# First modulation by pairs of feature tiles, q from two token tiles, written engine orders up to the end of q

## The chip, the cores and the metric

The kernel runs on one core of a Trainium2 chip. Its engines are TensorE (PE in the profile, with PEld for the loads of its stationary operand), VectorE (DVE), ScalarE (ACT), GpSimd (POOL) and SyncE (SP), which here issues nearly all transfers. The metric is the time of one execution in microseconds (us); for a set of runs the median is given.

## The reference

One layer of a hybrid backbone is computed for 128 context tokens and 512 latent tokens, width 1024, all in float32. Cut to what matters here:

```
mod = silu(cond) @ w_ada + b_ada            # cond: c for latent, c_ctx for context tokens
sh1, sc1, g1, sh2, sc2, g2 = split(mod, 6)
h = rms(x, norm_mix) * (1 + sc1) + sh1
q, k, v, gb, gc, u = split(h @ w_in, ...)   # 512, 128, 128, 512, 512, 512 columns
attn = attention(rope(rms(q)), [ctx_k, rope(rms(k))], [ctx_v, v])
y_conv = gb * conv3(gc * u)
x = x + g1 * (concat(rms(attn), rms(y_conv)) @ w_out)
h2 = rms(x, norm_ffn) * (1 + sc2) + sh2
x = x + g2 * ((silu(gate) * up) @ w_down)   # gate, up = split(h2 @ w_gate_up)
```

The part that is changed runs from the first transfer to the last product of q: it needs `sh1` and `sc1`, `h`, and `h @ w_in` for the first 512 columns.

## The kernel before

The 640 tokens are five token tiles of 128: 0 to 3 are latent, 4 is the context. The 1024 features are eight feature tiles of 128, called k below. The products that carry precision are made of three: an operand is split into a high part of type fp32r and a low part that is the difference (`wh` and `wl` for weights, `hH` and `hL` for h), and `mm3` (lines 154 to 156) adds high × high, high × low and low × high. A *step* of q is one `mm3` of one feature tile and one token tile, 512 columns wide, into the token tile's own PSUM bank; there are 40.

Before q's first step, each x tile is loaded, squared and summed (`x_norm`: ScalarE), scaled by its inverse root (GpSimd's power, VectorE's multiply), transposed (`xT_do`: TensorE, eight times 128 by 128) and copied to `xT` by ScalarE and VectorE. The first modulation is computed for one feature tile at a time: `ada1_load` brings the 128 scale and 128 shift columns of `w_ada`, in two halves of four row blocks, into `af` tiles (four buffers); `ada1_mm` multiplies them with the conditioning vectors, four products side by side in strips of 32 columns (line 379), into 256 columns of PSUM, and copies the result to `res`; `ada1_mod` adds the strips with two small products against `sel` (line 428), and `mod_evict` makes the coefficients `modA` and `modB` on VectorE. `h_do` then computes `hF` from `xT` (ScalarE for the latent tokens, VectorE for the context) and splits it into `hH` (ScalarE) and `hL` (VectorE).

q's weights come as four loads of two feature tiles (`wf`, three buffers), split by ScalarE and VectorE into `wh` and `wl` (four buffers each, lines 150 and 151). k's and v's two loads and the conv's loads use the same rings.

The order of the work is set in several ways. TensorE's is the order in which the program is written, from the preparation on. On VectorE, ScalarE and GpSimd, a written order holds only for the string `P1PRE`; behind it, and on SP throughout, a scheduler places each instruction by priority (`early(...)` raises or lowers it). The letters of `P1PRE`: `rN` normalise x tile N, `xN` transpose it, `aN` the modulation's products for feature tile N, `mN` the small ones, `hNc` h for feature tile N, `qNt` a step, `w` a split of q's weights, `v`, `p`, `c` small constants. For feature tiles 1 to 7 the string `P1SEQ` says what stands in each round: the small products of the next feature tile, its h, the modulation's products of the one after, and the five steps.

After q, its five banks are copied to `of` (ScalarE four, VectorE one), and k, v, attention, conv, output projection and the feed-forward part follow.

Of the kernel before, what the change touches and what calls it, by code (L numbers as in the profile page):

```python
# [36 lines left out]
XTE = [0, 1, 0, 1, 1, 1, 0, 1, 1, 0]  # L37
# [39 lines left out]
AO = 6  # L77
# [9 lines left out]
LOADS = [0, 0, 0, 0, 2, 1, -1, 0, 3, 3, 2, 2]  # L87
# [3 lines left out]
def build(ctx, tc, x_prompt, x_sample, c, cache_k, cache_v, c_ctx, norm_mix, norm_ffn, w_ada, b_ada,  # L91
# [163 lines left out]
    def W(key):  # L255
        p = place[key]
        while not in_pre[0] and stream_at[0] < len(order):
            nxt = order[stream_at[0]][0][0]
            ahead = AO if nxt == "o" else AOP if nxt in ("g", "u", "op") else AHEAD
# [52 lines left out]

    crow = T("crow", (16, P))
# [3 lines left out]
    def ada1_load(k):  # L317

        out = []
        for h in range(2):  # L320
            wf = T("af", (P, 4, 2, P), F32, AFB)
            for i, col in enumerate((D + k * P, k * P)):
                sp.dma_start(wf[:, :, i], wa[:, 4 * h:4 * h + 4, col:col + P])
            out.append(wf)
            yield
        ada1[k] = out
        yield
# [13 lines left out]
    loads = itertools.chain(*(ada1_load(k) for k in range(KD)))  # L341
    ada1 = {}
# [70 lines left out]
    def ada1_mm(k):  # L413
        while k not in ada1:
            ada1_next(1)
        rp = PB((P, 256), tag="c")
        for h, wf in enumerate(ada1[k]):
            for i in range(4):
                cond_mm(rp, 4 * h + i, wf[:, i].rearrange("p a b -> p (a b)"))
        res = T("res", (P, 256), F32, 2)  # L420
        dve.tensor_copy(res, rp)
        ada1[k] = res

    def ada1_mod(k):
        res = ada1.pop(k)
        mp = PB((P, 2, 1, 2))
        for i in range(2):
            pe.matmul(mp[:, i, 0], res[:, i * P:(i + 1) * P], sel[:, 0:2], start=True, stop=True)
        mod_evict(0, k, 1, mp[:, 0], mp[:, 1])
# [3 lines left out]
    def xT_do(t):  # L433

        both = PS2() if t < XB else None
        tps = [both[:, i] if t < XB else PB() for i in range(2)]
# [4 lines left out]
        if t < XB:  # L441
            for k in range(KD):
                turn(k)
        for i, tp in enumerate(tps):
            if t >= XB:
                for k in range(4):
                    turn(4 * i + k)
# [8 lines left out]
    def h_do(k, cc):  # L456
        if k not in hF:
            hF[k] = T("hF", (P, TOK), F32, 2)
        s = (slice(0, 512), slice(512, TOK))[cc]
        a, b = modA[0][:, k, cc:cc + 1], modB[0][:, k, cc:cc + 1]  # L460
        if cc == 0:
            act.activation(hF[k][:, s], xT[:, k, s], AF.Identity, bias=b, scale=a)
        else:
            dve.tensor_scalar(hF[k][:, s], xT[:, k, s], a, b, ALU.mult, ALU.add)
        if k == 0:
            split(hH[k][:, s], hL[k][:, s], hF[k][:, s])
        elif cc == 1:
            split(hH[k], hL[k], hF[k])

    pe_order = tc.manual_schedule(engines={mybir.EngineType.PE})  # L470
    pe_order.__enter__()
# [16 lines left out]
    qacc = []  # L488

    def q_mm(k, t):  # L490
        if not qacc:
            qa, qb = PS2(), PS2()
            qacc.extend([qa[:, 0], qa[:, 1], qb[:, 0], qb[:, 1], PB(tag="c")])
# [18 lines left out]
    steps = {"r": x_norm, "c": late_consts, "w": lambda i: load_split(*deferred.pop(0)), "p": lambda i: rows2_load(), "x": xT_do, "v": lambda i: (vec_do, vec2_do)[i](), "m": ada1_mod, "a": ada1_mm}  # L512
    pre_order = tc.manual_schedule(engines={mybir.EngineType.DVE, mybir.EngineType.Activation, mybir.EngineType.Pool})
    pre_order.__enter__()
# [809 lines left out]
```

## Time and profile before

| | |
|---|---|
| median of three runs | 760.89 us (759.51 to 763.18) |
| the profiled execution | 762.66 us, of which the span from first to last instruction is 760.9 us |
| mean granted clock of TensorE | 0.993 of full speed |
| PE busy | 739.5 us, 97% of the span |
| DVE, ACT, POOL busy | 73%, 49%, 6% of the span |
| moved by DMA | 84.52 MB, 111 GB/s in the mean |

The page divides the span into 40 slices of 19 us; the changed part fills the first three and a little of the fourth. A row of a timeline gives the start, the duration, the engine, the line, what is written and read, and in brackets how long the engine was idle before and what ended that. Several alike are put together (x8).

### The profile page before, as it was taken

Reading aid. Unit: us, or ns where it says so; the run is one execution under the profiler, and the core shown is the slowest. Engines: PE = TensorE matmul, PEld = TensorE weight load, DVE = VectorE, ACT = ScalarE, POOL = GpSimd, SP = SyncE. Lnnn points to the kernel's source line nnn. Section 1 sums busy time; section 2 is a strip of 40 time slices with the busy share of each in tenths; the row PEclk is TensorE's granted clock in tenths of the full one; section 3 lists DMA queues with packets and bytes.
Section 4 is the critical chain, followed back from the end, with each engine's and each line's share of the span. In section 5 each row is a group of like instructions: output and inputs, shape, how many; then the busy total and the mean of one; then the engine's idle time right before and its main releaser. Section 6 shows DMA issues by size and latency. Waiting matters only on the chain.

```text
span 760.9 us, 11844 instructions
## 1 busy us (share of the span) xinstructions
PE 739.5 (97%) x4580; PEld 664.6 (87%) x4580; DVE 552.7 (73%) x1003; ACT 369.6 (49%) x715; POOL 43.1 (6%) x73
## 2 busy tenths in 40 slices
PE   4999999999999999999999999999999999999997
PEld 3768888989998887899898789998889998899986
DVE  5556987676666797779879678884578866788653
ACT  5345867666656444765552135553125541255410
POOL 3104301011010110100000000000000000000000
PEclk9899999999999999999999999999999999999999
DMA  9985132522433363031335223223113132222312
GB/s 289 293 233 158 38 118 91 173 91 91 160 104 93 130 249 111 1 112 56 86 111 179 83 62 103 79 89 113 53 56 110 58 112 67 73 86 82 111 56 84
DMA packets 102349, 84.52 MB, mean 111 GB/s; under 512 B 4526, under 2 KB 82674, under 8 KB 102292
## 3 DMA queue, kind: packets, MB, share of 16 engines
q1 hardware_dynamic: 100980, 83.39, 35.5%
q8 instruction: 36, 0.59, 0.3%
q10 hardware_dynamic: 1056, 0.26, 0.2%
q0 software_dynamic: 256, 0.11, 0.1%
q14 instruction: 21, 0.17, 0.1%
HBM read 79.68 MB, written 2.75 MB: 108 GB/s over the span
## 4 chain that ended last, share of the span: by engine, by line
PE 82%; DVE 8%; DMA 3%; ACT 2%; SPq 2%; issue 1%; POOL 1%; DVEq 0%; POOLq 0%
PE pf L154 17%; PE pf L156 16%; PE pf L155 16%; PE pc L677 3%; PE pc L678 3%; PE pc L679 3%; PE po L834 3%; PE ps L791 2%; PE ph L154 2%; PE pt L817 2%; PE ph L155 2%; PE ph L156 2%; PE pc L379 2%; DMA af<-in_w_ada_dram 2%; DMA wf<-in_w_gate_up_dram 1%
## 5 line engine op out<-in xcount | busy, mean ns | idle before, releaser
L150 ACT ACTIVATE wh<-wf 128x1024 fp32r<-128x1024 f32 (+1 forms) x76 | 64.1, 843 | 95.7 <-PE pf L156 61.8
L154 PE MATMUL pf<-wh,gT 128*128 128x512 f32 (+1 forms) x225 | 88.1, 392 | 0.0
L155 PE MATMUL pf<-wl,gT 128*128 128x512 f32 (+1 forms) x225 | 87.7, 390 | 0.0
L156 PE MATMUL pf<-wh,gT 128*128 128x512 f32 (+1 forms) x225 | 87.7, 390 | 0.0
L151 DVE TENSOR_TENSOR wl<-wf,wh 128x1024 fp32r<-128x1024 f32 (+1 forms) x42 | 49.4, 1175 | 29.1 <-ACT wh L150 26.3
L677 PE MATMUL pc<-hH,wh 128*128 128x320 f32 x192 | 61.1, 318 | 0.0
L678 PE MATMUL pc<-hL,wh 128*128 128x320 f32 x192 | 59.4, 310 | 0.0
L679 PE MATMUL pc<-hH,wl 128*128 128x320 f32 x192 | 59.4, 309 | 0.0
L155 PEld LDWEIGHTS pf<-wl,gT 128*128 128x128 f32 x225 | 42.2, 188 | 10.0 <-issue 0.2
L154 PEld LDWEIGHTS pf<-wh,gT 128*128 128x128 f32 x225 | 42.2, 188 | 9.9 <-ACT wh L150 0.2
L156 PEld LDWEIGHTS pf<-wh,gT 128*128 128x128 f32 x225 | 42.2, 188 | 9.8
L154 PE MATMUL pf<-T,wh 128*128 128x320 f32 x160 | 49.7, 311 | 0.5 <-ACT u L1154 0.5
L155 PE MATMUL pf<-T,wl 128*128 128x320 f32 x160 | 49.5, 309 | 0.0
L155 PE MATMUL pf<-T,wh 128*128 128x320 f32 x160 | 49.5, 309 | 0.0
L156 PE MATMUL pf<-T,wh 128*128 128x320 f32 x160 | 49.5, 309 | 0.0
L154 PE MATMUL pf<-T,wl 128*128 128x320 f32 x160 | 49.5, 309 | 0.0
L156 PE MATMUL pf<-T,wl 128*128 128x320 f32 x160 | 49.5, 309 | 0.0
L154 PE MATMUL pf<-B,wl 128*128 128x320 f32 x152 | 47.3, 311 | 0.1
L156 PE MATMUL pf<-B,wl 128*128 128x320 f32 x152 | 47.1, 310 | 0.0
L155 PE MATMUL pf<-B,wl 128*128 128x320 f32 x152 | 47.0, 309 | 0.0
L1233 DVE TENSOR_TENSOR dm<-pf,g 128x512 f32<-128x512 f32 (+1 forms) x41 | 27.7, 675 | 22.8 <-PE pf L156 22.6
L154 PE MATMUL pf<-B,wh 128*128 128x320 f32 x136 | 42.3, 311 | 1.5 <-DVE cu L1183 1.5
(293 smaller groups left out, 2023.9 us busy)
## 6 DMA issues: line engine op xcount, KB each, us to landing
wf<-in_w_gate_up_dram SPq DMA_DIRECT2D x44, 512.0 KB, 4.0
aw<-in_w_ada_dram SPq DMA_DIRECT2D x24, 512.0 KB, 4.7
wf<-in_w_down_dram SPq DMA_DIRECT2D x20, 512.0 KB, 3.4
wf<-in_w_in_dram SPq DMA_DIRECT2D x18, 512.0 KB, 6.1
af<-in_w_ada_dram SPq DMA_DIRECT2D x32, 256.0 KB, 6.0
x<-in_x_sample_dram SPq DMA_DIRECT2D x8, 512.0 KB, 4.8
wf<-in_w_out_dram SPq DMA_DIRECT2D x8, 512.0 KB, 3.9
wf<-in_w_ada_dram SPq DMA_DIRECT2D x8, 512.0 KB, 3.7
```

What stands on the lines that cost most here:

```text
L150: act.activation(hi, src, AF.Copy)
L151: dve.tensor_tensor(lo, src, f32(hi), ALU.subtract)
L154: pe.matmul(out, lh, rh, start=start, stop=False, skip_group_check=more)
L155: pe.matmul(out, lh, rl, start=False, stop=False, skip_group_check=more)
L156: pe.matmul(out, ll, rh, start=False, stop=stop, skip_group_check=more)
L379: pe.matmul(out[CG * g:CG * (g + 1)], cp[:, k], w, start=(k < 4), stop=(k >= KD - 4), skip_group_check=True)
L677: pe.matmul(acc, wh[:, k], hH[k][:, c0:c0 + n], start=(k == 0), stop=False)
L678: pe.matmul(acc, wh[:, k], hL[k][:, c0:c0 + n], start=False, stop=False)
L679: pe.matmul(acc, wl[:, k], hH[k][:, c0:c0 + n], start=False, stop=(k == KD - 1))
L791: pe.matmul(s2[:, g, :320], q, kk[:, v, P + g * 320:P + (g + 1) * 320], start=(i == 0), stop=(i == 1))
L834: pe.matmul(ov, w, x[:, i].rearrange("p a q -> p (a q)"), start=(g == 0 and i == 0 and n == 0), stop=(last and i == len(kts) - 1 and n == 1))
L1233: dve.tensor_tensor(dm, ps[:, :n], g2[cc][:, oc], ALU.mult)
```

## The change

- **Modulation by pairs.** `ada1_load` brings the columns of two feature tiles at once (256 columns each of scale and shift), in halves of 1 MB; `ada1_mm` is written half by half and fills 512 columns of PSUM; `ada1_mod` makes the coefficients of both tiles with four small products. There are four pairs; the `af` ring still has four buffers, each twice as large.
- **h.** ScalarE writes `hH` directly from `xT`, and VectorE computes `hF` for all tokens and then `hL`. For feature tiles 0 and 1 this is done in parts: tokens 0 and 1 together (`a`), token tiles 2 (`b`), 3 (`c`) and 4.
- **Order of loads and steps.** Two x tiles come first, then the first pair's weights, q's first weights, and the other three x tiles. q begins with token tiles 0 and 1 of feature tiles 0 and 1.
- **Idle products.** `spin` multiplies the identity by itself into the last bank of q, whose first real step starts it afresh: 14 ahead of all, 2 and 4 around the modulation's first half, and 14 ahead of q.
- **Written orders.** SP, VectorE, ScalarE and GpSimd keep the written order to the end of q as TensorE does. In it the split of q's next weights stands behind the h of the pair.
- k's and v's loads are issued in the last pair's round, cache loads behind them.

The core of the diff:

```diff
-P1SEQ = 'm h a 0 1 2 3 4'
-P1PRE = ('r0 r1 r2 x0 r3 x1 v0 x2 a0 w0 x3 m0 r4 h00 a1 q02 q01 x4 q00 m1 h01 h10 a2 q03 h11 p0 q04 c0')
-XB = 3
+P1SEQ = 'q00 q01 q02 a0 q03 q04 a1 q10 m h0 h1 q11 q12 q13 q14'
+P1PRE = ('d9 d5 r0 r1 v0 x0 x1 d2 a00 d4 a01 m0 w0 h0a d9 d5 h1a r2 r3 q00 q01 q10 q11 x2 h0b r4 x3 h1b a20 q02 h0c q12 h1c q03 '
+         'x4 q13 a21 h04 h14 m2 w0 q04 q14 h2* h3* p0 c0')
...
-LOADS = [0, 0, 0, 0, 2, 1, -1, 0, 3, 3, 2, 2]
+LOADS = [0, 0, 2, -1, 0, 0, 0, 2, -1]
...
+    sp_order = tc.manual_schedule(engines={mybir.EngineType.SP, mybir.EngineType.PE})
+    sp_order.__enter__()
+    pre_order = tc.manual_schedule(engines={mybir.EngineType.DVE, mybir.EngineType.Activation, mybir.EngineType.Pool})
+    pre_order.__enter__()
...
     def ada1_load(k):
...
         for h in range(2):
-            wf = T("af", (P, 4, 2, P), F32, AFB)
+            wf = T("af", (P, 4, 2, 2 * P), F32, AFB)
             for i, col in enumerate((D + k * P, k * P)):
-                sp.dma_start(wf[:, :, i], wa[:, 4 * h:4 * h + 4, col:col + P])
+                sp.dma_start(wf[:, :, i], wa[:, 4 * h:4 * h + 4, col:col + 2 * P])
...
+    def ada1_mm(k, h):
+
+        if h == 0:
+            ada1_ps[k] = PB((P, 512), tag="c")
+        wf = ada1[k][h]
+        for i in range(4):
+            cond_mm(ada1_ps[k], 4 * h + i, wf[:, i].rearrange("p a b -> p (a b)"))
+        if h == 1:
+            ada1[k] = T("res", (P, 2, 2, P), F32, 1)
+            dve.tensor_copy(ada1[k], ada1_ps.pop(k).rearrange("p (i f q) -> p i f q", i=2, f=2))
 
     def ada1_mod(k):
         res = ada1.pop(k)
-        mp = PB((P, 2, 1, 2))
-        for i in range(2):
-            pe.matmul(mp[:, i, 0], res[:, i * P:(i + 1) * P], sel[:, 0:2], start=True, stop=True)
-        mod_evict(0, k, 1, mp[:, 0], mp[:, 1])
+        mp = PB((P, 2, 2, 2))
+        for f in range(2):
+            for i in range(2):
+                pe.matmul(mp[:, i, f], res[:, i, f], sel[:, 0:2], start=True, stop=True)
+        mod_evict(0, k, 2, mp[:, 0], mp[:, 1])
...
+    HS = {"a": slice(0, 256), "b": slice(256, 384), "c": slice(384, 512), "l": slice(0, 512), "4": slice(512, TOK)}
+
+    def h_do(k, part):
...
+        for x in "l4" if part == "*" else part:
+            s, cc = HS[x], int(x == "4")
+            g, b = modA[0][:, k, cc:cc + 1], modB[0][:, k, cc:cc + 1]
+            act.activation(hH[k][:, s], xT[:, k, s], AF.Identity, bias=b, scale=g)
+            dve.tensor_scalar(hF[k][:, s], xT[:, k, s], g, b, ALU.mult, ALU.add)
+            if part != "*":
+                dve.tensor_tensor(hL[k][:, s], hF[k][:, s], f32(hH[k][:, s]), ALU.subtract)
+        if part == "*":
+            dve.tensor_tensor(hL[k], hF[k], f32(hH[k]), ALU.subtract)
...
+    def spin(n):
+
+        for _ in range(n):
+            pe.matmul(qacc[4][:, :P], ident, ident, start=True, stop=True)
...
+    for k in range(2, KD, 2):
+        if k + 2 < KD:
+            ada1_next(2)
+            load_next(True)
+        else:
+            load_next()
+            load_next()
+        for x in P1SEQ.split():
+            if x[0] == "q":
+                q_mm(k + int(x[1]), int(x[2]))
...
+        if deferred:
+            load_split(*deferred.pop(0))
```

`xT_do` also transposes every tile through two single banks, four transposes and a copy each, where the first three tiles had two banks at once and eight transposes ahead of the copies; ScalarE now copies each tile's first half and VectorE the second.

On VectorE, before, where the coefficients of feature tile 5 are made (`modt`, `modB`, `modA`); `wl_413` is the low part of q's weights for tiles 6 and 7, and `wl_407` that for tiles 4 and 5:

```order
L151 TENSOR_TENSOR wl_407<-wf_404,wh_406 128x1024
L501 COPY vec_143<-pt_481 128x20
L402 TENSOR_TENSOR modt_493<-pt_490,vec_143 128x2
L406 TENSOR_TENSOR modB_32_147<-pt_490,vec_143 128x2
L403 TENSOR_TENSOR modA_30_145<-modt_493,nb_144 128x2
L151 TENSOR_TENSOR wl_413<-wf_410,wh_412 128x1024
L464 TENSOR_SCALAR hF_497<-xT_165,modA_30_145,modB_32_147 128x128
L421 COPY res_511<-pc_502 128x256
L151 TENSOR_TENSOR hL_46_161<-hF_497,hH_38_153 128x640
```

And now, where the coefficients of tiles 4 and 5 are made; `wl_497` is the low part of q's weights for these same tiles:

```order
L424 COPY res_458<-pc_443 128x512
L404 TENSOR_TENSOR modt_468<-pt_463,vec_134 128x4
L405 TENSOR_TENSOR modA_26_136<-modt_468,nb_135 128x4
L408 TENSOR_TENSOR modB_28_138<-pt_463,vec_134 128x4
L465 TENSOR_SCALAR hF_472<-xT_156,modA_26_136,modB_28_138 128x512
L465 TENSOR_SCALAR hF_472<-xT_156,modA_26_136,modB_28_138 128x128
L469 TENSOR_TENSOR hL_42_152<-hF_472,hH_34_144 128x640
L465 TENSOR_SCALAR hF_478<-xT_156,modA_26_136,modB_28_138 128x512
L465 TENSOR_SCALAR hF_478<-xT_156,modA_26_136,modB_28_138 128x128
L469 TENSOR_TENSOR hL_43_153<-hF_478,hH_35_145 128x640
L151 TENSOR_TENSOR wl_497<-wf_432,wh_496 128x1024
```

The weights' low part moved from ahead of a tile's h, by a round or more, to behind the h of both tiles of its own pair; and `hF` of 512 columns is new on VectorE.

On TensorE, now, from the last steps of feature tile 3 to the first of tile 4, which are the first to read `wh_496` and `wl_497`:

```order
L154 MATMUL ps_158<-wh_396,hH_33_143 128x512
L155 MATMUL ps_158<-wl_397,hH_33_143 128x512
L156 MATMUL ps_158<-wh_396,hL_41_151 128x512
L154 MATMUL pc_159<-wh_396,hH_33_143 128x512
L155 MATMUL pc_159<-wl_397,hH_33_143 128x512
L156 MATMUL pc_159<-wh_396,hL_41_151 128x512
L154 MATMUL ps_157<-wh_496,hH_34_144 128x512
L155 MATMUL ps_157<-wl_497,hH_34_144 128x512
L156 MATMUL ps_157<-wh_496,hL_42_152 128x512
```

Between the steps of two feature tiles stood small products and the next modulation's products in every round before; between tiles 3 and 4 there is nothing now.

On TensorE at the start, before (`pt` and `ps` are PSUM banks, `pc` a modulation's sums):

```order
L367 MATMUL pt_135<-ident_76,crow_73 128x16
L439 MATMUL ps_197<-ident_76,x_91 128x128 x8
L439 MATMUL ps_216<-ident_76,x_93 128x128 x8
L386 MATMUL pt_227<-ident_76,rows_86 128x64
L439 MATMUL ps_232<-ident_76,x_95 128x128 x8
L379 MATMUL pc_243<-af_99,cp_84 32x256 x4
```

and now (`pc_159` is the bank that the idle products write):

```order
L369 MATMUL pt_126<-ident_80,crow_77 128x16
L477 MATMUL pc_159<-ident_80 128x128 x14
L388 MATMUL pt_193<-ident_80,rows_90 128x64
L441 MATMUL pt_198<-ident_80,x_95 128x128 x4
L441 MATMUL pt_199<-ident_80,x_95 128x128 x4
L441 MATMUL pt_210<-ident_80,x_97 128x128 x4
L441 MATMUL pt_211<-ident_80,x_97 128x128 x4
L477 MATMUL pc_159<-ident_80 128x128 x2
L381 MATMUL pc_224<-af_99,cp_88 32x512 x4
L477 MATMUL pc_159<-ident_80 128x128 x4
L381 MATMUL pc_224<-af_102,cp_88 32x512 x4
```

Fourteen idle products stand ahead of the transposes, the third and fourth tile's transposes stand behind q's first steps, and the modulation's products are 512 columns wide.

More of the change, by code (lines that the diff above doesn't have):

```diff
@@ L340, in build @@
     xs = []
-    loads = itertools.chain(*(ada1_load(k) for k in range(KD)))
-    ada1 = {}
+    loads = itertools.chain(*(ada1_load(k) for k in range(0, KD, 2)))
+    ada1, ada1_ps = {}, {}
     def x_load():
@@ L510, in rows2_load @@
         pool.dma_start(rows2[8:20, :], conv_w[0].rearrange("w (r q) -> (w r) q", q=P))
[L512 to L514 removed]
+    steps = {"r": x_norm, "c": late_consts, "w": lambda i: load_split(*deferred.pop(0)), "p": lambda i: rows2_load(), "x": xT_do, "d": spin, "v": lambda i: (vec_do, vec2_do)[i](), "m": ada1_mod, }
     in_pre[0] = True
@@ L529, in build @@
     sp.dma_start(cv, cache_v[0, 0])
[L530 to L543 removed]
+    sp_order.__exit__(None, None, None)
+    pe_order = tc.manual_schedule(engines={mybir.EngineType.PE})
+    pe_order.__enter__()
     qraw = [None] * NT
```

78 lines of the change are left out of this document (22 added, 56 removed).

## The prediction

> **What bounds the kernel now.** I read the page first, then the windows of the first 120 us, the chain of waits, and the rows of TensorE, VectorE and ScalarE in order of time.
>
> ```profile
> span 760.9 us, 11844 instructions
> ...
> PEclk9899999999999999999999999999999999999999
> ```
>
> TensorE is the bound from the second slice on, at full clock, and the change leaves its rows after q as they were. So what counts is when q ends, and how soon behind it the next chain starts. In the windows the mean clock (the column behind POOL) shows two stretches where TensorE is slow:
>
> ```profile
> core 0: us, PE busy (x) PEld busy (x) DVE busy (x) ACT busy (x) POOL busy (x), PEclk, DMA share, GB/s
> ...
> 20.00:25.00 5.00, 5.00 (x23) 3.85 (x16) 1.12 (x3) 0.00 (x0) 1.38 (x3) 0.51 1.16 284
> ...
> 40.00:45.00 5.00, 3.48 (x19) 2.36 (x16) 3.62 (x9) 2.64 (x4) 0.00 (x0) 0.70 1.04 292
> ```
>
> The transfers are busy throughout, at some 288 GB/s. In the chain, a transfer of the first modulation's weights ends last before 41.6 us:
>
> ```profile
> 32.67 8.76 DMA af<-in_w_ada_dram
> ```
>
> TensorE's own rows (start, us, line, output and inputs, columns):
>
> ```profile
> 3.21 0.25 PE L367 MATMUL pt<-ident,crow 16*128 16x16 f32 x1 [3.21 <-ACT crow L365]
> ...
> 7.86 3.60 PE L439 MATMUL ps<-ident,x 128*128 128x128 f32 x16 [4.40 <-DVE x L478]
> ...
> 11.60 1.09 PE L439 MATMUL ps<-ident,x 128*128 128x128 f32 x8
> ...
> 20.46 0.79 PE L154 MATMUL ps<-wh,hH 128*128 128x512 f32 x1
> ...
> 23.19 1.87 PE L439 MATMUL pt<-ident,x 128*128 128x128 f32 x8
> ...
> 33.58 0.50 PE L428 MATMUL pt<-sel,res 128*128 128x2 f32 x4
> 34.01 1.07 PE L379 MATMUL pc<-af,cp 128*32 128x256 f32 x16
> ...
> 35.58 0.40 PE L156 MATMUL ps<-wh,hL 128*128 128x512 f32 x1
> ...
> 38.39 0.39 PE L156 MATMUL pc<-wh,hL 128*128 128x512 f32 x1
> ...
> 41.57 0.75 PE L379 MATMUL pc<-af,cp 128*32 128x256 f32 x8 [1.52 <-DMA af<-in_w_ada_dram]
> 42.25 0.79 PE L154 MATMUL ps<-wh,hH 128*128 128x512 f32 x1
> ...
> 45.40 0.40 PE L155 MATMUL ps<-wl,hH 128*128 128x512 f32 x1
> ...
> 64.59 0.40 PE L156 MATMUL pc<-wh,hL 128*128 128x512 f32 x1
> 64.82 0.28 PE L154 MATMUL pc<-wh,hH 128*128 128x256 f32 x1
> ```
>
> q is 40 steps (8 feature tiles by 5 token tiles) of three products. From 35.58 to 38.39 there are 12 products, 0.234 us each, so a step is 0.70 us. q starts at 20.46 at half clock, reaches the 11th step (tile 2, tokens 0) at 35.58 and ends at 64.82. Seven products between 42.25 and 45.40 take 3.15 us where 1.64 would do: that slow stretch costs 1.5, on top of 1.5 of waiting for the weights.
>
> **The change, part by part.**
>
> *Transfers.* The first q product needs 3.67 MB in both kernels (four tiles of x, 1.05 MB of modulation weights and 0.52 of q's; now two tiles of x and 2.10 MB). Of before, this had landed when ScalarE could split the weights:
>
> ```profile
> 14.38 1.06 ACT L150 ACTIVATE wh<-wf 128x1024 fp32r<-128x1024 f32 x1 [2.29 <-DMA wf<-in_w_in_dram]
> ```
>
> I take the same 14.4. Behind it, at 288 GB/s, the eight weight halves of 1.05 MB and what stands between them are in by 32.6 us (the fifth), 36, 42 and 45 (the eighth); by the times below they are wanted at 37, 40, 49 and 52. So the wait of 1.5 us for the weights goes, and transfers bound nothing. SP has half as many issues for these weights. Its wait for a free buffer (four, each now twice as large) is for halves used long before, except the eighth, which waits for the fourth's products at 31, with three transfers queued ahead.
>
> *Up to the first q product.* Fourteen idle products of 128 columns now stand ahead of everything. No row shows one. Eight transposes of that width take 1.09 at full clock and 1.87 at half, about 0.11 and 0.21 each; the f32 products here show two rows each (L379: 8 calls, 16 rows), so an idle product takes 0.21 at full clock, at least 0.11 (one pass) and at most 0.43. They start at 3.5 and end between 6.5 and 9.5. The clock starts low (of the row at 7.86, the second tile's eight, from about 9.5, took two us), so I take 9.0. The two tiles' transposes, through two single banks with copies between, take 2.5: 11.6. Then two idle (0.4), half the weights (0.9), four idle (0.9), the other half (1.0): 14.8. A half is four calls of 512 columns, as the later modulations have them:
>
> ```profile
> 99.38 1.07 PE L379 MATMUL pc<-aw,cp 128*32 128x512 f32 x8
> ```
>
> The copy of 512 columns (0.7), the small products of two feature tiles (four calls, eight rows; the row at 33.58 has four rows in 0.50, 0.43 to the next: 0.9) and 14 idle ones (3.0) bring q's start to 19.5. VectorE and ScalarE are done about then: coefficients 16.9, weight split 18.1, two halves of h 19.4. That is 1.0 us earlier than 20.46, and at full clock, where before paid half clock up to 25.
>
> *The first ten steps.* VectorE's prices, from the groups by shape up to 66 us (busy, mean ns):
>
> ```profile
> L151 DVE TENSOR_TENSOR wl<-wf,wh 128x1024 fp32r<-128x1024 f32 x7 | 8.6, 1224 | 3.3 <-ACT wh L150 3.2
> ...
> L462 ACT ACTIVATE hF<-xT,modB,modA 128x512 f32<-128x512 f32 x8 | 6.5, 811 | 9.4 <-DVE modA L403 8.6 <-DVE ms L162 0.8
> L151 DVE TENSOR_TENSOR hL<-hF,hH 128x640 fp32r<-128x640 f32 x7 | 5.8, 823 | 1.8 <-ACT hH L150 1.8
> ...
> L478 DVE TENSOR_SCALAR x<-x,rs 128x1024 f32<-128x1024 f32 x5 | 3.8, 753 | 2.8 <-POOL rs L164 2.7
> ...
> L464 DVE TENSOR_SCALAR hF<-xT,modA,modB 128x128 f32<-128x128 f32 x8 | 2.7, 342 | 0.1
> ...
> L452 DVE COPY xT<-pt 128x512 f32<-128x512 f32 x2 | 1.4, 688 | 3.3 <-PE pt L439 3.3
> ```
>
> hF of 512 columns was ScalarE's and is now VectorE's, with no row: between 0.34 (128 columns) and 0.75 (1024), on the line through both 0.52. Rows of one engine overlap by some 0.08. TensorE's work up to the 11th step is 10 × 0.70 + 3 tiles × 1.0 + two halves 1.9 + 0.9 = 12.8. Between lie four waits: 0.5 for the copy of a transpose's bank, 0.9 for VectorE (normalising x3 and x4, copies, then the h of tokens 2), 0.7 for the copy of the second pair's sums, and 1.3 at the 11th step. There TensorE has the small products (0.9) and two steps (1.4) left and wants the third product 0.5 later, at 2.8; VectorE has the h of tokens 4 and the coefficients (1.45), the weight split (1.15), hF (0.44 + 0.26) and hL (0.8): 4.1. Sum: 19.5 + 12.8 + 3.4 = 35.7, against 35.58. The early start is spent on waits.
>
> *The other 29 steps.* After 35.58 before needed 29.2 to q's end (64.82): 20.4 of steps, three tiles' weights (3.0), four small products (1.8), the 1.5 + 1.5 above, and 1.0 of a transpose, switching and the rest of the 11th step. After has 20.4, four halves (4.0), two pairs' small products (1.8) and 0.4: 26.6. To this come two waits, ahead of steps 21 and 31, where q's next weights enter. Between the small products and those steps TensorE has four steps, 2.8 us. VectorE's queue has the coefficients, both tiles' hF and hL, and behind them the weight split. From four rows of small products to the use of their coefficients it is 0.92 us; with eight, 1.35:
>
> ```profile
> 28.53 0.50 PE L428 MATMUL pt<-sel,res 128*128 128x2 f32 x4
> ...
> 29.06 0.16 DVE L402 TENSOR_TENSOR modt<-pt,vec 128x2 f32<-128x2 f32 x1 [1.00 <-PE pt L428]
> ...
> 29.45 0.81 ACT L462 ACTIVATE hF<-xT,modB,modA 128x512 f32<-128x512 f32 x1 [0.56 <-DVE modA L403]
> ```
>
> So the split ends 1.35 + 2 × (0.44 + 0.26 + 0.08 + 0.74) + 1.23 = 5.6 after the small products begin. TensorE wants it at 0.9 + 2.8 + 0.23 (the first product needs only ScalarE's half, ready at 4.4) = 3.9. Each wait is 1.7, together 3.4: 30.0. Where before waited for transfers and at half clock, after waits for VectorE. q ends at 35.7 + 30.0 = 65.7 against 64.8: +0.9.
>
> *Behind q.* ScalarE's row before:
>
> ```profile
> 65.02 1.06 ACT L150 ACTIVATE wh<-wf 128x1024 fp32r<-128x1024 f32 x1 [3.74 <-PE pc L156]
> 65.99 2.04 ACT L551 ACTIVATE of<-ps 128x512 f32<-128x512 f32 x4
> 67.90 0.30 ACT L584 ACTIVATE ph<-pc 128x128 f32<-128x128 f32 x1
> ```
>
> A weight split that needed q's end stood ahead of q's four copies; now it stands behind them, and the copies start as their banks finish. The next step, ph, needs the first k and v products (24 of half the width, 0.12 us each, 2.9 behind q's end), so where it came 3.1 behind it, only 0.2 is gained. Rope tables, cache loads and k and v splits move by a few us with slack.
>
> The sum is +0.9 − 0.2 = +0.7 against the profiled execution's 762.66 (its span 760.9 and 1.8 around it): 763.4. The runs shown have the median 760.89, so I forecast 761.6; alone, with an idle product at 0.11 to 0.25 and hF at its ends (0.2 each way, four times), this case reaches 759 to 763. A measurement of this kernel can tell about 0.5%, 3.8 us, from no change.
>
> **The rivals.**
>
> *The waits are covered: faster.* If VectorE keeps up everywhere, the waits of 0.9, 1.3 and twice 1.7 go: 761.6 − 5.6 = 756.0. For it: the overlap on VectorE may be larger than 0.08, and two waits alone make 3.4. Against: the split alone is 1.2 and stands last. Chance 0.13.
>
> *The clock falls in the waits: slower.* The last three waits lie in a stretch of q that I reckon at full clock. In the trace one 1.5 us wait, with light products around it, was enough to halve the clock at 42.25; full-width products were absent from 38.6 to 42.25. Each fall costs some 1.6: with three 4.8, 766.4; with two, 764.8. Against: here full-width products stand close on both sides. It decides when a wait and the light products beside it grow to some 3.6 us. Chance 0.22.
>
> The Trainium skill's page "TensorE: Matmul & The Clock Gate" (Part 1) says the gate closes after an idle window of about 3.4 us, free-running; the trace agrees, with 3.6 us free of full-width products. By that rule waits of 1.7 us close nothing, and the time would stay at 761.6.
>
> *The first conv weights are late.* Their split now stands ahead of q's copies on both engines, and their transfer behind a modulation's. If it lands after 63.5, copies and ph slip by up to 1.0: 762.6. Chance 0.10.
>
> *The idle products do not lift the clock.* Then the second fourteen take 6.0 and q starts 3.0 later: 764.6, still within what counts as no change. Against: by then TensorE has been busy for most of 12 us, and the row at 11.60 shows full clock with less. Chance 0.07.
>
> **How the numbers follow.** The forecast has 0.48 and, with the last two rivals, 0.65 lies within 0.5%; faster by more has 0.13 (the covered waits, 0.64%), slower by more 0.22 (two falls 0.51%, three 0.72%). The range reaches into both outer rivals, 757.0 to 766.0; about half of each, 0.17, falls beyond.
>
> **What would show it.** Right: first q product at 19.5 us, at 0.23 us spacing; the 11th step near 35.7; two waits of about 1.7 us on VectorE's wl ahead of steps 21 and 31; no wait for af after 30 us; q's end at 65.7. Wrong: gaps below 0.5 there, clock rows of 0.5 between 33 and 62 us, or q's copies held by a conv split.

## The result, and the profile after

The changed kernel takes 769.46 us in the median of five runs (767.51 to 770.70), the kernel before 760.51 us in five runs beside it (759.51 to 763.18). The ratio is 1.0109, with a 95% interval of 1.0081 to 1.0137: slower by 8 to 9 us. The prediction had 761.6 us and a range up to 766.0. The profiled execution of the changed kernel took 769.46 us, its median. Each run has its own mean granted clock, and it matters below: the five runs are 767.51 and 767.67 us at 1.000, 769.46 at 0.997, 770.62 and 770.70 at 0.995. From the page of the profiled execution:

```profile
span 767.7 us, 11840 instructions
...
PEclk9999999999999999999999999999999999999999
...
PE 85%; DVE 8%; ACT 3%; DMA 1%; issue 1%; POOL 1%; SPq 0%; ACTq 0%; DVEq 0%; POOLq 0%
```

The last line is the share of each engine in the chain that ended last; transfers have 1% of it. The windows of the changed kernel (columns as in the prediction's windows: length, then busy time and count of PE, PEld, DVE, ACT, POOL, then clock, DMA share and GB/s):

```profile
20.00:25.00 5.00, 4.75 (x30) 3.82 (x28) 2.90 (x8) 2.21 (x6) 1.10 (x2) 1.00 1.08 357
...
40.00:45.00 5.00, 5.00 (x31) 2.37 (x30) 0.97 (x3) 0.00 (x0) 0.00 (x0) 1.00 0.26 82
45.00:50.00 5.00, 3.92 (x18) 2.71 (x17) 3.85 (x10) 3.24 (x5) 0.00 (x0) 1.00 0.00 0
...
60.00:65.00 5.00, 3.16 (x13) 2.01 (x13) 4.66 (x8) 4.34 (x7) 0.87 (x1) 1.00 0.24 54
```

Both half-clock stretches of before (0.51 and 0.70 in the first two of these slices) are gone. Transfers run at 357 GB/s where they ran at 284, and stand still from 45 to 50 us. But TensorE is idle in the later slices, which it was not before. Its rows in order of time:

```profile
17.19 3.37 PE L477 MATMUL pc<-ident 128*128 128x128 f32 x28
20.32 0.48 PE L154 MATMUL ps<-wh,hH 128*128 128x512 f32 x1
...
28.90 0.50 PE L156 MATMUL ps<-wh,hL 128*128 128x512 f32 x1 [0.87 <-DVE hL L467]
...
33.55 1.02 PE L431 MATMUL pt<-sel,res 128*128 128x2 f32 x8 [0.91 <-DVE res L424]
...
38.15 0.50 PE L156 MATMUL ps<-wh,hL 128*128 128x512 f32 x1 [1.15 <-DVE hL L469]
...
44.45 1.05 PE L431 MATMUL pt<-sel,res 128*128 128x2 f32 x8
...
48.02 0.40 PE L156 MATMUL pc<-wh,hL 128*128 128x512 f32 x1
49.31 0.50 PE L154 MATMUL ps<-wh,hH 128*128 128x512 f32 x1 [0.90 <-ACT wh L150]
50.91 0.50 PE L155 MATMUL ps<-wl,hH 128*128 128x512 f32 x1 [1.10 <-DVE wl L151]
...
62.29 0.50 PE L154 MATMUL ps<-wh,hH 128*128 128x512 f32 x1 [0.74 <-ACT wh L150]
63.90 0.50 PE L155 MATMUL ps<-wl,hH 128*128 128x512 f32 x1 [1.10 <-DVE wl L151]
...
70.77 0.28 PE L154 MATMUL pc<-wh,hH 128*128 128x256 f32 x1
```

q starts at 20.32, at full clock (20.46 before), reaches the 11th step's third product at 38.15 (35.58) and ends at 70.77 (64.82): of the 6.8 us between the two profiled spans, 5.95 are there at q's end. The step that enters new weights stands at 48.25 when its turn comes, gets its first product at 49.31 and its second, which needs `wl`, at 50.91 where 48.49 was due: 2.4 us. It is the same again at 63.90. What VectorE did meanwhile:

```profile
46.01 0.80 DVE L465 TENSOR_SCALAR hF<-xT,modA,modB 128x512 f32<-128x512 f32 x2
47.25 0.83 DVE L469 TENSOR_TENSOR hL<-hF,hH 128x640 fp32r<-128x640 f32 x1 [0.43 <-ACT hH L464]
47.99 0.80 DVE L465 TENSOR_SCALAR hF<-xT,modA,modB 128x512 f32<-128x512 f32 x2
48.89 0.82 DVE L469 TENSOR_TENSOR hL<-hF,hH 128x640 fp32r<-128x640 f32 x1
49.64 1.22 DVE L151 TENSOR_TENSOR wl<-wf,wh 128x1024 fp32r<-128x1024 f32 x1
```

The weight split is last in the queue, as written, and its weights had landed long before: the windows show no byte moved from 45 to 50 us.

The remaining 0.85 us lies behind q, where one stretch runs at half clock in this execution; of the kernel before, the same work (6 us earlier) does not. TensorE's rows ahead of this stretch come 5.9 us later than before, those behind it 7.4 us later: it costs 1.5 us, of which 0.6 comes back by the end. The changed kernel first, before second:

```profile
80.40:83.80 3.40, 2.34 (x20) 1.86 (x19) 3.40 (x14) 2.89 (x9) 0.70 (x1) 0.98 0.13 39
83.80:87.20 3.40, 3.40 (x16) 3.40 (x16) 2.86 (x9) 3.29 (x11) 1.94 (x1) 0.51 0.00 0
```

```profile
76.00:79.00 3.00, 2.31 (x21) 2.17 (x20) 3.00 (x12) 2.77 (x7) 1.38 (x2) 1.00 0.07 22
79.00:82.00 3.00, 3.00 (x26) 3.00 (x25) 2.33 (x7) 2.34 (x9) 1.26 (x1) 1.00 0.00 0
```

### The profile page after: what moved, and what is told of

Its sections match the earlier page's. It is cut to its first block, busy times and chain, and to the rows that moved or that the text cites. A ratio compares the mean times of both kernels' runs of the same rounds, so it can differ in the third digit from the quotient of the medians.

```text
span 767.7 us, 11840 instructions
## 1 busy us (share of the span) xinstructions
PE 747.3 (97%) x4584; PEld 668.8 (87%) x4584; DVE 558.1 (73%) x1003; ACT 368.5 (48%) x719; POOL 44.0 (6%) x73
## 4 chain that ended last, share of the span: by engine, by line
PE 85%; DVE 8%; ACT 3%; DMA 1%; issue 1%; POOL 1%; SPq 0%; ACTq 0%; DVEq 0%; POOLq 0%
PE pf L156 17%; PE pf L155 17%; PE pf L154 17%; PE pc L688 3%; PE pc L689 3%; PE pc L690 3%; PE pc L381 2%; PE po L845 2%; PE ph L154 2%; PE ph L155 2%; PE ph L156 2%; PE ps L802 2%; PE pt L828 2%; PE pc L477 1%; DVE wl L151 1%
## 5 line engine op out<-in xcount | busy, mean ns | idle before, releaser
L155 PE MATMUL pf<-wl,gT 128*128 128x512 f32 (+1 forms) x225 | 87.7, 390 | 0.0
L154 PE MATMUL pf<-wh,gT 128*128 128x512 f32 (+1 forms) x225 | 87.6, 389 | 0.0
L151 DVE TENSOR_TENSOR wl<-wf,wh 128x1024 fp32r<-128x1024 f32 (+1 forms) x42 | 49.9, 1189 | 27.8 <-ACT wh L150 25.0
L155 PEld LDWEIGHTS pf<-wl,gT 128*128 128x128 f32 x225 | 42.2, 188 | 10.3 <-issue 0.2
L154 PEld LDWEIGHTS pf<-wh,gT 128*128 128x128 f32 x225 | 42.2, 188 | 9.9 <-ACT wh L150 0.2
L154 PE MATMUL pf<-T,wh 128*128 128x320 f32 x160 | 49.6, 310 | 0.5 <-ACT u L1165 0.5
L155 PE MATMUL pf<-T,wl 128*128 128x320 f32 x160 | 49.4, 309 | 0.0
L154 PE MATMUL pf<-T,wl 128*128 128x320 f32 x160 | 49.4, 309 | 0.0
L155 PE MATMUL pf<-T,wh 128*128 128x320 f32 x160 | 49.4, 309 | 0.0
L154 PE MATMUL pf<-B,wl 128*128 128x320 f32 x152 | 47.1, 310 | 0.0
L155 PE MATMUL pf<-B,wl 128*128 128x320 f32 x152 | 47.0, 309 | 0.0
L154 PE MATMUL pf<-B,wh 128*128 128x320 f32 x136 | 42.2, 310 | 1.5 <-DVE cu L1194 1.5
```

The costliest lines, as they stand in the source:

```text
L151: dve.tensor_tensor(lo, src, f32(hi), ALU.subtract)
L154: pe.matmul(out, lh, rh, start=start, stop=False, skip_group_check=more)
L155: pe.matmul(out, lh, rl, start=False, stop=False, skip_group_check=more)
```

## The experiments

My theory: q is paced by the order written for VectorE and ScalarE, above all by the place of the weight split. Rivals: the wait would only change its name; the idle products; the clock; the transfers. Each kernel ran beside the kernel before on the same chip; the medians of the kernel before were 760.76 in the first four comparisons, 760.82 in the next four, 760.58 in the last four.

**1. The split ahead of the pair's h, in the rounds.** `SOQ` holds the priorities of the four splits.

```diff
-SOQ = [0, -300, -300, -300]
-P1SEQ = 'q00 q01 q02 a0 q03 ...'
+SOQ = [0, 0, 0, 0]
+P1SEQ = 'q00 q01 w q02 a0 q03 ...'
...
+            elif x[0] == "w":
+                if deferred:
+                    load_split(*deferred.pop(0))
...
-        if deferred:
-            load_split(*deferred.pop(0))
```

> The changed kernel, with q's weight split of rounds 2 and 3 written ahead of the pair's coefficients and h on VectorE and ScalarE (its lowered priority taken away, since that pushes it behind them). Theory (q is paced by the order written for VectorE and ScalarE): the two waits of 2.4 us ahead of steps 21 and 31 go and nothing new comes in their place, q ends at 70.8 - 4.8 = 66.0 us and the time falls by 4 to 5 us against the changed kernel, to about 764.7. Rival (TensorE waits for h of the pair, or for something else beside the split): the wait stays and only changes its name, to h or to the coefficients, and q's end stays at 70 to 71 us, the time near 769. Rival (the loss lies behind q, by the clock): q's end moves to 66 but the time stays within 1 us of 769.

764.71 us, 1.0043 of before (1.0028 to 1.0057). VectorE and TensorE in this kernel's profile:

```profile
39.98 1.22 DVE L151 TENSOR_TENSOR wl<-wf,wh 128x1024 fp32r<-128x1024 f32 x1
```

```profile
48.03 0.40 PE L154 MATMUL ps<-wh,hH 128*128 128x512 f32 x1
48.26 0.40 PE L155 MATMUL ps<-wl,hH 128*128 128x512 f32 x1
...
65.85 0.28 PE L154 MATMUL pc<-wh,hH 128*128 128x256 f32 x1
```

The split is done at 41.2 us, the step that waited 2.4 us follows its forerunner at 0.23, and q ends 4.9 us earlier. The theory holds, in q's end to 0.2 us; nothing took the waits' place. It holds at equal clock too: the four runs at 1.000 take 763.0 to 763.2 us, the changed kernel's two 767.5 and 767.7.

**2. The split ahead of the coefficients at q's start, and ahead of the last tokens' copies at the 11th step.**

```diff
-... a01 m0 w0 h0a ... h1c q03 x4 q13 a21 h04 h14 m2 w0 q04 ...
+... a01 w0 m0 h0a ... h1c w0 q03 x4 q13 a21 h04 h14 m2 q04 ...
```

> The changed kernel, with the split of q's first weights written ahead of the first coefficients, and that of the second pair's weights ahead of the copies and h of the last tokens. Theory (q is paced by the written order): the first q product comes about 1 us earlier, at 19.2 to 19.5 us, the wait of 1.15 us at the 11th step's third product goes, and q ends about 2 us earlier, at 68.5 to 69; the time is 767 to 768. Rival (what paces the start is the weights' landing or TensorE's small products): the first q product stays at 20.3, and the ten steps up to the 11th take as long as before, so that q's end stays at 70 to 71 us.

768.75 us, 1.0104 (1.0086 to 1.0122). In its profile:

```profile
20.34 0.48 PE L154 MATMUL ps<-wh,hH 128*128 128x512 f32 x1
...
37.24 0.50 PE L156 MATMUL ps<-wh,hL 128*128 128x512 f32 x1 [0.51 <-DVE hL L469]
...
63.00 0.80 PE L155 MATMUL ps<-wl,hH 128*128 128x512 f32 x1 [1.10 <-DVE wl L151]
...
71.39 0.28 PE L154 MATMUL pc<-wh,hH 128*128 128x256 f32 x1
```

This holds in half. The wait at the 11th step falls from 1.15 to 0.51, but q's start does not move: the fourteen idle products and TensorE's other work ahead of it set it, as the rival said. q's end even came later, since in this execution the wait of the third round was followed by a half-clock stretch:

```profile
59.50:62.92 3.42, 1.69 (x7) 0.81 (x5) 3.32 (x6) 3.42 (x6) 0.00 (x0) 1.00 0.28 64
62.92:66.33 3.41, 3.33 (x8) 2.65 (x9) 3.41 (x5) 0.52 (x1) 3.06 (x3) 0.50 0.61 172
```

**3. Without the idle products** (all `d` letters taken out of `P1PRE`).

> The changed kernel without its idle products. Theory (they hold the clock at full, but 14 of them stand ahead of the transposes and 14 ahead of the first q product): the first q product comes no earlier, since VectorE and ScalarE set its time with the coefficients, split and h, at 19.5 to 20.3 us, but at half clock for some 3 to 5 us, as in the kernel before; the time is 1.5 to 2.5 us above the changed kernel's, 771 to 772. Rival (the idle products cost more than they bring): the first product comes 1 us or more earlier and the time is below 768.5. Rival (they bring nothing): within 0.7 us of 769.5.

771.28 us, 1.0136 (1.0112 to 1.0160), and in its profile

```profile
18.23 0.50 PE L154 MATMUL ps<-wh,hH 128*128 128x512 f32 x1 [1.22 <-ACT hH L464]
```

```profile
21.00:24.00 3.00, 3.00 (x11) 2.31 (x11) 1.57 (x3) 0.00 (x0) 0.56 (x2) 0.55 1.09 357
...
51.00:53.00 2.00, 1.75 (x4) 1.46 (x5) 0.20 (x1) 0.00 (x0) 0.00 (x0) 0.51 0.26 22
```

The time is as expected, though the start was not: q starts 2.1 us earlier and loses it again at half clock. The medians put the idle products at some 1.8 us of gain, but the two intervals overlap; leaving all of them out does not bring the loss back.

**4. Both moves of the split together** (edits 1 and 2).

> The two moves of q's weight splits together: ahead of the coefficients and h at q's start, at the 11th step and in rounds 2 and 3. Theory (q is paced by the written order): the gains add up, q ends at 63.5 to 64.5 us, about where the kernel before ends it (64.8), and the time is 762 to 763, within 0.5% of the kernel before. Rival (each wait is replaced by the next one on VectorE, whose queue has the same work whatever its order): q ends at 67 or later and the time is 766 or more.

762.80 us, 1.0030 (1.0019 to 1.0042), q starting at 20.40 and ending at 65.28. The time is as expected, q's end 0.8 us later than that. With the splits early, 6.7 us of the loss are back in the median (6.0 by the ratios). Of the 1.9 us beyond experiment 1 only 0.6 lies at q's end (65.28 after 65.85). At a clock of 0.999 or 1.000 seven of nine runs take 762.5 to 762.9, where experiment 1's take 763.0 to 763.2; the rest of the 1.9 is the clock of the median run (0.995 there, 0.999 here), not the order.

**5. Fewer idle products on top of that.**

```diff
-'d9 d5 r0 r1 v0 x0 x1 d2 a00 d4 a01 w0 m0 h0a d9 d5 h1a ...
+'d9 d5 r0 r1 v0 x0 x1 a00 a01 w0 m0 h0a d5 h1a ...
```

> The version with all weight splits early, with fewer idle products: the first fourteen stay, the six around the first half of the weights go, and of the fourteen ahead of the first q product five stay. Theory (with the splits early, q's start is paced by the idle products themselves, which end at 20.4 us where h is ready at about 18.9, and by the weights' products behind them): the first q product comes at 17.7 to 18.7 us at full clock, q ends 1 to 2.5 us earlier, at 63 to 64.3, and the time is 760.5 to 762. Rival (nine idle products fewer let the clock fall): half clock for some microseconds behind q's first product, and the time is 763 or more. Rival (the first ten steps wait for later tokens anyway, whose normalisation is not earlier): q starts earlier but the 11th step stays at 37, and the time stays at 762.8.

761.28 us, 1.0007 (0.9996 to 1.0018).

```profile
17.77 0.50 PE L154 MATMUL ps<-wh,hH 128*128 128x512 f32 x1 [0.45 <-ACT hH L464]
...
35.05 0.50 PE L156 MATMUL ps<-wh,hL 128*128 128x512 f32 x1 [0.52 <-DVE hL L469]
...
63.02 0.28 PE L154 MATMUL pc<-wh,hH 128*128 128x256 f32 x1
```

q starts 2.6 us earlier than with all of them, at full clock, and ends 2.3 earlier; 1.5 of it arrives in the time. In the median this mended kernel takes what the kernel before takes. At a clock of 0.999 or 1.000 it is still behind: 760.0 to 760.3 us, against 758.6 to 759.7 for the kernel before in the same comparison. The medians meet because the kernel before loses more to half clock: its runs there have a mean clock of 0.996, these 0.998.

**6. Idle products in the two waits**, ten ahead of step 21 and ten ahead of step 31 of the changed kernel.

```diff
+        if k > 2:
+            fill = PB()
+            for _ in range(10):
+                pe.matmul(fill[:, :P], ident, ident, start=True, stop=True)
         for x in P1SEQ.split():
```

> The changed kernel with ten more idle products ahead of step 21 and of step 31, about 2.4 us each, into a bank of their own: the waits for the weight split are filled. Theory (the waits cost their own length and sometimes a clock fall besides): q ends within 0.5 us of 70.8, no row at half clock stands between 45 and 70 us, and the runs lie close together at the lower end of the changed kernel's, 767.5 to 768.5. Rival (the clock falls in the light stretch behind q, whatever stands in the waits): runs of 770 and more stay, and the median stays at 769.5. Rival (the clock has no part in it): no change at all.

768.69 us in four runs, 1.0110 (1.0093 to 1.0126): three at 768.5 to 768.7, one at 769.97. The profile has no half clock and ends q at 70.99. That leans to the theory, but the interval covers the changed kernel's ratio; inconclusive, and below 1 us either way. The three runs at a clock of 1.000 take 768.5 to 768.7 us, the changed kernel's two 767.5 and 767.7: the idle products cost about 1 us of their own. One run in four has a lower clock here, three in five there, too few to tell whether they hold it.

**7. Short rows.** The first modulation's weights in rows of 512 bytes, with twice as many transfers.

```diff
-                sp.dma_start(wf[:, :, i], wa[:, 4 * h:4 * h + 4, col:col + 2 * P])
+                for f in range(2):
+                    sp.dma_start(wf[:, :, i, f * P:f * P + P], wa[:, 4 * h:4 * h + 4, col + f * P:col + f * P + P])
```

> The changed kernel with the first modulation's weights fetched as before, 128 columns by a transfer (rows of 512 bytes in place of 1024, twice as many transfers), into the same tiles. Theory (the row length sets the rate: 349 to 381 GB/s with 1024 bytes, 284 to 292 with 512): the rate up to 40 us falls to about 290 GB/s, q starts 1 to 2 us later, TensorE waits again for weights in the first or second round, and the time is 2 to 6 us above the changed kernel's, 771.5 to 775. Rival (the rate does not hang on the row length, or the transfers have slack everywhere): within 1 us of 769.5.

771.16 us, 1.0134 (1.0115 to 1.0154).

```profile
20.00:25.00 5.00, 4.75 (x30) 3.93 (x29) 2.90 (x7) 2.21 (x6) 1.10 (x2) 1.00 1.17 291
...
51.00:53.00 2.00, 1.94 (x5) 1.59 (x6) 0.01 (x1) 0.00 (x0) 0.00 (x0) 0.59 0.24 36
```

The rate falls from 357 to 291 GB/s in this slice (from 353 to 302 between 20 and 40 us). Rows half as long and twice as many transfers came together, so no run tells which of the two sets it. But q starts at 20.48, TensorE waits nowhere for weights, and what is longer up to q's end in this profile is a half-clock stretch behind the wait at 51 us. The interval overlaps the changed kernel's, and at about equal clock no difference is left: 769.25 and 769.36 us at 0.998 here, 769.46 at 0.997 there. The half of the theory on the time falls: the transfers have slack here even at the old rate.

**8. The kernel before with idle products and nothing else of the change**: eight around the first small products, four between the halves of feature tile 1's weights, six between those of tile 5.

```diff
-'... w0 x3 m0 r4 ...
+'... w0 x3 d4 m0 d4 r4 ...
...
+            if h == 1 and k in IDLE:
+                spin(IDLE[k])
```

> The kernel before with idle products and nothing else of the change: eight around the first small products, four between the halves of the second feature tile's weights, six between those of the sixth (where its trace shows the second half-clock stretch, 42.25 to 45.4 us). Theory (idle products hold the clock, and the kernel before is paced by its transfers up to 41.6): of the two half-clock stretches the first gives back at most 0.5 us, since the weights still land at 41.6, and the second 1.5; the time is 758.8 to 760 against 760.8. Rival (idle products only take TensorE's time): 761 to 763. Rival (both stretches count in full): 757 or less.

762.64 us, 1.0028 (1.0014 to 1.0041): slower, with its number in the range of the rival. The profile says otherwise on the way there:

```profile
62.26 0.28 PE L155 MATMUL pc<-wh,hH 128*128 128x256 f32 x1
```

```profile
75.00:80.00 5.00, 5.00 (x30) 5.00 (x29) 4.43 (x12) 3.81 (x12) 1.94 (x1) 0.66 0.01 3
```

q ends 2.6 us earlier than in the profile of before, with no row at half clock from 14 us up to there (a line more in this kernel makes L155 of what is L154 there). And no wait of TensorE for the modulation's weights is left, of which the kernel before had 3.7 us in three:

```profile
PE pc L379 <- DMA af<-in_w_ada_dram: 3.7, 3, 1.5
```

That transfers set the pace of the kernel before up to 41.6, as I had held, is not borne out; that they had no part in it is not shown either. Groups of idle products stand in the place of all three waits and are about as long (1.14 us for 1.06, 1.16 for 1.09, 1.53 for 1.52), and experiment 9, the same up to q's end, still has a wait of 0.6 us for these weights, at 28 us. From its first product to its end q takes 40.9 us instead of 44.4; by the rows, the two half-clock stretches in q had cost that much (2.0 and 1.5). The lead was lost behind q: the spans are 760.6 and 760.9.

The idle products cost time of their own as well. At a clock of 1.000 the runs of this kernel take 761.8 and 762.0 us, those of the kernel before in the same comparison 759.2 to 759.7. Where these 2.4 us lie is open: the profile of the kernel before has half clock, and there is none of it without.

**9. The same with seven more idle products in the light stretch behind q**: `idle` multiplies the identity by itself into a bank that is not in use yet, two products ahead of each of the first two turns of k, one and two ahead of the halves of q's first turn.

```diff
+        idle(2, (1, 2))
...
+            idle(1 + g, (3, 4))
```

> The kernel before with idle products in q, as in the run before of that kind, and with seven more in the light stretch behind q. That run ended q 2.7 us earlier than the kernel before and was 1.8 us slower all the same; its profile shows a half-clock stretch at 75 to 79 us. Theory (q's lead was lost to the clock behind q): without that stretch the time is 759.5 to 761. Rival (the lead is lost in waits for other engines further behind): the half-clock stretch goes and the time stays at 762 or more.

762.42 us, 1.0034 (1.0019 to 1.0049). The same slice, now at full clock:

```profile
75.00:80.00 5.00, 4.74 (x39) 4.55 (x39) 4.46 (x13) 4.54 (x14) 2.39 (x2) 1.00 0.02 3
```

The half clock goes and the time stays: the rival. Between the profiles, the lead over before shrinks from 2.4 us at q's end to 1.7 at the first transposes, 1.3 at 88 us and 0.5 at the end; the waits that stand at the first two places are for ScalarE (0.6 and 0.4 us). Part of the first place is GpSimd's: k's head norm still comes 3.4 us behind q's end, but the next one 1.44 us behind it instead of 0.73. VectorE waits 0.33 us between them for GpSimd's rope table, which ends at 67.1 because its transfer landed only at 63.8; the chain that ended last runs through that transfer there, and no longer through q. What takes the lead from 1.7 to 0.5 is not shown.

**10. and 11. The mended kernel (5) with the same seven idle products, and with the second pair's weights earlier instead.**

```diff
-... h0c q12 h1c w0 q03 x4 q13 a21 h04 h14 m2 q04 ...
+... h0c a21 q12 h1c w0 m2 q03 x4 q13 h04 h14 q04 ...
```

> The version with all weight splits early and fewer idle products, and seven more idle products in the light stretch some 10 us behind q's end (ahead of the first transposes of k and q). Theory (there the clock falls in many executions, for about 3.4 us at a time, which costs 1.1 to 1.7 us): no row at half clock is left between 70 and 85 us, the runs of 761 and more become rare, and the median falls by 0.5 to 1.2 us, from 761.3 to 760.1 to 760.8. Rival (the idle products delay the transposes by as much as they save): 761 to 762.

> The version with all weight splits early and fewer idle products, and the second pair's second half of weights and its small products moved ahead among the first ten steps (behind the 5th and the 6th instead of behind the 8th). Theory (the first ten steps still wait for the written order: 0.90 for the copy of the pair's sums and 0.52 for its h): both waits go, the 11th step's third product comes at 33.5 to 34.3 us instead of 35.05, and the time falls by 0.8 to 1.5 us, to 759.8 to 760.5. Rival (the pair's weights have not landed, or VectorE has no room for the work earlier): the wait moves to the 6th step or to the weights, and the time stays within 0.4 us of 761.3.

762.61 us, 1.0016 (1.0003 to 1.0028), and 760.87 us, 1.0005 (0.9996 to 1.0013). The first holds the clock behind q (1.00 in every slice from 70 to 85 us) and still comes out 1.3 us above kernel 5 (0.7 by the ratios, whose intervals overlap). Its profiled execution has half clock inside q instead (0.73 from 30 to 35 us) and a new wait at 389 us, of 0.77 for VectorE; kernel 5's has neither. The clock does not account for it: at 0.999 or 1.000 its runs take 761.0 to 762.1 us, kernel 5's 760.0 to 760.3. Why seven products at 70 us cost that is open. The second only moved its waits, as its rival said (0.58 and 0.69 us earlier on, 0.64 at the 11th step): the 11th step's third product came at 35.46, q's end at 63.43, both 0.4 later than in kernel 5, with less than its own uncertainty gained.

**12. Both together.**

> Both of these together: the pair's second half earlier, and the idle products behind q. Theory: the gains add up, 758.6 to 759.8, faster than the kernel before by 0.1 to 0.3%. Rival (q's lead is lost behind q): 760.5 or more.

762.10 us, 1.0020 (1.0010 to 1.0031): the rival. No version beats the kernel before; in the median 5 and 11 equal it.

## Why the prediction was wrong

The mechanism was named: where the kernel before waited for transfers and at half clock, the changed one waits for VectorE's weight split, and experiment 1 shows that it is worth 4.8 us. It had the waits; what failed are the sizes of the terms, all to one side, and the base that they were added to. Of the 7.9 us between 761.6 and 769.46:

- **The two waits: 1.4.** Put at 1.7 each, measured 2.4. The step that failed here is the sum on VectorE's queue: 5.6 us from the small products to the end of the split, measured 6.4 (44.45 to 50.86). It left out that `hL` waits for ScalarE's `hH` (0.43) and let eight small products delay the coefficients by 1.35 where 1.56 passed.
- **The first ten steps: 1.6.** 16.2 us was the term, 17.8 the time (20.32 to 38.15). The waits came out near their values (1.0 for 0.9, 0.91 for 0.7, 1.36 for 1.3, 0.25 for 0.5); 0.5 is a slip in the sum: 38.15 is the 11th step's third product, and the two products ahead of it (0.23 each) are not among the 12.8 us of work. The other 1.0 is small gaps: the first product behind narrow ones or behind a wait takes 0.31 to 0.34 us to the next instead of 0.23, and 0.53 pass ahead of the 11th step, whose operand load waits for ScalarE's `hH`. A price per instruction does not hold these.
- **The rest of the other 29 steps: 1.2.** 27.8 us without the waits instead of 26.6, by the same gaps at each entry and exit of a modulation half.
- **q's start: 0.8.** 20.3 us instead of 19.5. The idle products' price was right (fourteen in 3.37 us, 0.24 each, for 0.21); the first small products began at 16.30, where the sum has 15.5, so the whole miss was there by then, in TensorE's work on the first weights and the copy behind it. VectorE's way there was not what counted: experiments 2 and 5 show that TensorE's own idle products set the start.
- **Behind q: 1.0.** 0.2 was to be gained; 0.85 was lost, with the half clock at 83.8 us. The prediction put a clock fall there at nothing, without a reason: its rival looked for falls in q's waits alone.
- **From the profiled execution to the median: 1.8.** I took 1.77 us off because before's profile was that much above its median. The changed kernel's profile is its median. Before's profiled execution has two half-clock stretches and a mean clock of 0.993. The runs of the kernel before beside the experiments, at 0.992 to 1.000, show that its median has less of them: in the comparison of experiments 5 to 8 the runs around the median of 760.82 have 0.996 and 0.997, those at 0.993 take 761.8 and 762.2, those at 1.000 take 759.2 to 759.7. So most of the 1.77 is half clock, and the sum had already taken the half clock of that profile out (the 1.5 at 42.25 and the slow start of q): it was counted twice. The changed kernel's median run, for its part, has a stretch of it.

*The rivals.* "The waits are covered" was wrong: they were longer than forecast. "The clock falls in the waits" gave the right side with a price of 1.6 each, but not this case's cause: in the changed kernel's profile the clock holds through all waits of q. It can fall there, as the profiles of experiments 2, 3 and 7 show, each time behind a wait of 2.4 us. The Trainium skill's page "TensorE: Matmul & The Clock Gate" (Part 1) gives a free-running window of about 3.4 us; the trace agrees on its length (62.92 to 66.33 at half clock in experiment 2) and on its dependence on phase, since the same wait closes the gate in one kernel and not in another. The rule as the prediction took it, that only an idle window closes the gate, is not what the traces show: the stretch that closed it in experiment 2 held 1.69 us of TensorE work in 3.42, and the one ahead of 42.25 us in the kernel before, which the prediction took to agree, held 1.88 us in 3.40. What waits of 1.7 us would do, no run shows. "The first conv weights are late" did not come true: k's head norm came 3.35 us behind q's end, 3.41 before. ScalarE did stand 3.84 us for these weights ahead of q's copies, but the copies began at 69.14, ahead of q's end. "The idle products do not lift the clock" was wrong: the second fourteen took 3.37 us where the first took 5.94, the clock is 1.00 in every slice of q, and without them (experiment 3) it is not.

*Transfers.* That they bound nothing after the change was right, and experiment 7 widens it: not even at 291 GB/s. That they alone bound the kernel before up to 41.6 us is not borne out, and how much they did is open (experiment 8).

## What to carry to other kernels

Where an order is written out by hand on the engines that feed the bound one, price each queue up to its last item, with its waits for the other feeder, and put an item whose inputs have long landed (here a weight split) ahead of those that are on the chain; its place in the rounds alone was worth 4.8 us, 0.6%. A sum of terms that are each priced from isolated rows comes out low when the changed code switches often between narrow and wide work: here such gaps made 2.2 us of the 5 by which q's end was missed. Look first at how far the profiled execution stands from the median, and at which clock stretches it contains, before it serves as the base of a sum. Then compare runs at equal granted clock: the medians call kernel 5 and the kernel before equal, the runs at 0.999 and 1.000 do not.

## What the runs showed of the hardware

- With the modulation's weights in rows of 1024 bytes the transfers ran at 349 to 357 GB/s in the slices from 20 to 40 us, with rows of 512 bytes and twice as many transfers at 287 to 316 (experiment 7), through the same queue into the same tiles. The slices hold q's weights as well.
- Half clock comes in pieces of about 3.4 us, and each cost about 1.5 us in the profiles here (at 42.25 us in the kernel before, at 83.8 in the changed one). The runs of a kernel fall into groups 1 to 2 us apart that go with the granted clock (the changed kernel: 767.5 and 767.7 at 1.000, 769.5 at 0.997, 770.6 and 770.7 at 0.995; experiment 1: 763.0 to 763.2 at 1.000, 764.7 to 765.2 at 0.995 and 0.997).
- A piece came behind 3.4 us in which TensorE was busy for 1.69 (a wait) and behind 3.4 in which it was busy for 2.34, with transposes and half-width products (behind q). It did not come in the changed kernel's 48 to 51 us, with 1.01 of 3.0 busy. If the pieces are cut by a fixed period, which is an inference from these traces, that wait was cut in two: counted back from 83.80 in steps of 3.41 us, it lies across the windows from 46.26 and from 49.67, with 2.52 and 2.31 us busy. The Trainium skill's page "TensorE: Matmul & The Clock Gate" (Part 4) says that transposes in TensorE's transpose mode do not count as busy in the same way; the stretch behind q fits that, but no run here separates transposes from the products beside them.
- Idle products held the clock (0.66 without and 1.00 with them from 75 to 80 us, experiments 8 and 9) and cost time besides: at a clock of 1.000 the kernel before takes 759.2 to 759.7 us, with eighteen idle products in it 761.8 and 762.0 (experiment 8).
